# Where layer 1's expert tokens come from: rows gathered by indirect DMA instead of one-hot matmuls, in a two-layer block with 16 experts

## Chip, cores and metric

One core of a Trainium2 chip runs the whole program as one launch. The metric is the device time of that launch in microseconds (us): before the change the median of 3 runs is 1519.34 us (1519.08 to 1524.59). In the profile PE is the matmul engine, DVE the vector engine, ACT the scalar engine, POOL is GpSimd, and SP is the engine that issues most loads.

## What is computed

The reference runs two layers over 512 latent tokens and 256 context tokens of width 1024. Each layer norms the tokens, projects them once into four head groups (pooling, grouped attention, Hyena, MLA), projects the joined result out and adds it. Then comes an expert-choice mixture of experts, which is the part that matters here:

```python
def expert_choice_ffn(h, w_router, w_gate, w_up, w_down):
    b, n, d = h.shape
    cap = EC_CAPACITY * n // N_EXPERTS          # 64 of 512 latent tokens, 32 of 256 context tokens
    aff = jax.nn.softmax((h @ w_router).astype(jnp.float32), axis=-1)
    gate, idx = lax.top_k(jnp.swapaxes(aff, 1, 2), cap)
    xg = jax.vmap(lambda hb, ib: hb[ib])(h, idx)
    a = jnp.einsum('becd,edf->becf', xg, w_gate)
    u = jnp.einsum('becd,edf->becf', xg, w_up)
    y = jnp.einsum('becf,efd->becd', jax.nn.silu(a) * u, w_down) * gate[..., None].astype(h.dtype)
    scatter = lambda ib, yb: jnp.zeros((n, d), h.dtype).at[ib.reshape(-1)].add(yb.reshape(-1, d))
    return jax.vmap(scatter)(idx, y)

for l in range(DEPTH):                          # DEPTH = 2; the context stream is dropped in the last layer
    ...
    x_new = x_new + g2 * expert_choice_ffn(modulate(rms_norm(x_new, norm2_g[l]), sh2, sc2), ...)
    if not last:
        xc = xc + modc[5] * expert_choice_ffn(modulate(rms_norm(xc, norm2_g[l]), modc[3], modc[4]), ...)
```

Each of the 16 experts has 6 MB of float32 weights in a layer (gate, up and down matrices of 1024 x 512).

## The kernel before

Python code with tiles and pools is traced once; a scheduler then puts each engine's instructions in a fixed order, and a tile that opens in room that another pool gave back waits for that pool's last readers. So the code sets the order only in part: where a tile lies, and how many buffers it has, move instructions as well.

**Routing.** `project_out` adds the mixed heads to the rows in `xn` (one pool, 128 x 1024 floats for each block of 128 tokens) and calls `route_part` for every block and quarter of the columns. It sums squares (L1347), makes the inverse norm `rs`, transposes, and adds to the logits (L1371, L1373). In layer 0 it also writes the normed rows to a scratch in DRAM: POOL multiplies the block (L1377, tile `xh`, one buffer) and issues a store of 512 KB (L1378). In layer 1 it returns before that. `route` then takes the top tokens by a chain of small DVE steps (L1435 to L1486) and gives gates, indices, `sidx` for the scatter and, in layer 0 alone, `gidx` for the gather.

**Picking the tokens.** A group is the tokens of two experts, 128 in all (of four for the context). There are two ways. `slot_matrix` and `gather_rows` pick on chip: PE broadcasts the indices (L1505), DVE builds a one-hot matrix (L1509), 64 matmuls of 128 x 128 multiply `xn` by it (L1521), DVE modulates what comes out (L1524). Or `gather` fetches 128 rows of 4 KB from the scratch by an indirect DMA on POOL's queue (L1573, tile `graw`, one buffer), PE transposes them in 8 steps (L1577), ACT and DVE modulate (`modulate`, L1497 and L1495). Layer 0 takes its first latent group on chip and the other seven, and all four of the context, by DMA. Layer 1 takes all eight on chip, so its `xn` stays until the end.

**Experts.** `expert(e)` is a generator; the loop in `moe` steps two of them in turn. Its PE work: 16 gate/up matmuls over the latent tokens, each of two passes (L1607, 32 in the profile), in layer 0 32 over the context tokens (L1618), transposes of the result (L1630, L1633), the down projections (L1642, in layer 0 also L1650). `glu` (L1593, L1594) and the copy to `hTm` (L1636) lie between. `scatter` makes `y` (L1584) and adds it into the output rows by an indirect DMA on POOL's queue (L1586). `nb` buffers for `y`, `sg` and `hTm`: 2 in layer 0, 1 in layer 1, where `y` and the one-hot matrix share one buffer (tag `lpart`).

**Weights.** `expert_loads` gives each expert six loads of 1 MB on SP's queue (L1544), in the order gate, up (first half), gate, up (second half), down, down, into slots of 1 MB: `ring2`, `ringt`, `ring3`, `ring4`. `SLOTS` says how many: layer 1 has 9 in ring2, 3 in ringt, 6 in ring3 and 2 in ring4, 20 in all. SP takes its queue in order, so one load that waits for its slot holds back all behind it.

Of the kernel before, what the change touches and what calls it, by code (L numbers as in the profile page):

```python
# [17 lines left out]
D = 1024  # L18
# [13 lines left out]
# ---------------------------------------------------------------- layout on the host  # L32
def blocks_(a):
    """rows in blocks of at most 128 partitions"""
    k, n = a.shape
    return np.ascontiguousarray(a.reshape(k // 128, 128, n).transpose(1, 0, 2).reshape(128, -1)).astype(np.float32)
# [138 lines left out]
# ---------------------------------------------------------------- the program  # L175
# the slots of the "ring2" pool in the order of their use, and how many slots "ring3" and "ring4" have
SLOTS = ([0, 1, 4, 2, 5, 3], 5, 4), ([0, 1, 2, 7, 8, 3, 4, 5, 6], 6, 2)
EARLY = 3, 9
LATE_STEPS = ((1, 0), (1, 2), (2, 0), (2, 2))
# which engine takes a step: vector (v), gpsimd (p) or scalar (a)  # L180
# [5 lines left out]
class Pipe:  # L186
    """side work, emitted a step at a time between the steps of the main work"""
# [18 lines left out]
class Block:  # L206
# [36 lines left out]
    def in_order(self):  # L243
        """the tensor engine takes what is traced inside in the order of the trace"""
# [11 lines left out]
    # ---- pieces  # L256
    def run(self):
# [33 lines left out]
        with self.pool("filt", side="right") as p:  # L291
# [3 lines left out]
            p.tile([128, 2048], F32, name="spare")  # the tiles after it lie clear of hT  # L295
# [29 lines left out]
    def open_layer(self, l):  # L325
        """the tables that a layer needs until its attention is done"""
# [26 lines left out]
    # ---- adaLN vectors  # L353
    def modulation(self, l, first=()):
        """a generator: one step for every 512 of the 6144 columns"""
# [45 lines left out]
    # ---- Hyena filters (weights only) -> spectra in DRAM  # L401
# [14 lines left out]
    def filter_mlp(self, p, k):  # L416
        """both layers at once, a layer on each half of the partitions"""
# [34 lines left out]
    def filters(self, scr, s):  # L452
        """the first layer's, in the given tiles"""
# [13 lines left out]
    def late_filters(self, tiles):  # L467
        """the second layer's, in tiles that the experts' weights take afterwards; a generator"""
# [24 lines left out]
    def filter_spectrum(self, tile, hid, w3, decay, tab, nb, n, spec, sqn, beside=False):  # L493
        """beside: the transforms leave the vector engine alone"""
# [51 lines left out]
    # ---- one layer  # L546
    def layer(self, l, npg, xh):
# [22 lines left out]
        def mla_out():  # L570
            """in the place of the rows of the grouped queries, when they are done"""
# [78 lines left out]
        if not last:  # L650
            mp = mg.__enter__()
# [3 lines left out]
        if not last:  # L655
            xpg.__exit__(None, None, None)
        rings["ring3"], rings["ring4"] = r3, r4g.__enter__()
        if last:
            mp = mg.__enter__()
        self.moe(l, mp, xgp, sel, xg0, A2, B2, last, W, load, len(slots) - early)  # L660
        for o in (xpg, r2g, mg, r4g, xgg) if last else (r2g, r4g, mg, xgg):
            o.__exit__(None, None, None)
# [1026 lines left out]
```

## Time and profile before

| | |
|---|---|
| runs, median (lowest to highest) | 1519.34 us (1519.08 to 1524.59) |
| profiled execution, span | 1520.5 us, 1.2 us above the median |
| PE busy | 1413.6 us, 93% of the span |
| DVE, ACT, POOL busy | 701.2, 493.1, 327.7 us |
| layer 0's experts, first gate matmul to last down matmul | 595.1 to 899.2 us |
| layer 1's experts, the same | 1267.0 to 1510.1 us |
| DMA | 339.7 MB, mean 223 GB/s |

The profile is of one execution; times inside it count from its start. "Busy" is the time in which an engine executes something. The chain of waits follows the work that ended last back from the last instruction. The windows view gives, for stretches of time, each engine's busy time, the clock granted to PE as a share of full speed (PEclk), and the busy share of the 16 DMA engines, which can read slightly over 1.

### The profile page before, as it was taken

What the parts mean: (1) busy time and instruction counts of PE and PEld (TensorE: products, weight loads), DVE (VectorE), ACT (ScalarE), POOL (GpSimd) and SP (SyncE); (2) the same over time, 40 slices, a digit from 0 to 9 for tenths busy, and PEclk for the clock granted to TensorE, in tenths of its full rate; (3) what the DMA queues carried; (4) which work ended last, traced back from release to release, by engine and by line L of the source; (5) the groups of instructions that cost most, each with busy time, mean ns of one, the idle gap of its engine ahead of it and who ended that gap; (6) DMA issues with size and microseconds to landing.
All of it is one profiled execution on the core that took longest, in us unless ns stands there. A gap on an engine that the chain in (4) does not pass through costs nothing.

```text
span 1520.5 us, 24869 instructions
## 1 busy us (share of the span) xinstructions
PE 1413.6 (93%) x9937; PEld 944.3 (62%) x9937; DVE 701.2 (46%) x1893; ACT 493.1 (32%) x1206; POOL 327.7 (22%) x344
## 2 busy tenths in 40 slices
PE   6999999897999989999999969999899969999996
PEld 2577787786778875444433327977778956445541
DVE  3555364778654465122222116685786462222221
ACT  5555333434763342010111026544357330000000
POOL 1420141355110133121221132042521000010101
PEclk8999999998999999999999989999899988999998
DMA  9556745011373078999999380123101766999992
GB/s 385 206 196 224 269 158 222 29 51 40 120 277 125 29 277 340 392 391 397 396 391 382 94 280 33 57 87 136 56 29 35 312 247 280 372 401 406 407 383 28
DMA packets 71012, 339.71 MB, mean 223 GB/s; under 512 B 6913, under 2 KB 22913, under 8 KB 36594
## 3 DMA queue, kind: packets, MB, share of 16 engines
q1 hardware_dynamic: 57488, 305.24, 51.2%
q0 software_dynamic: 11376, 25.89, 6.8%
q10 hardware_dynamic: 2034, 7.00, 1.2%
q8 instruction: 78, 1.28, 0.3%
q14 instruction: 36, 0.29, 0.1%
HBM read 313.50 MB, written 24.61 MB: 222 GB/s over the span
## 4 chain that ended last, share of the span: by engine, by line
PE 80%; DVE 10%; issue 3%; DMA 3%; ACT 2%; POOL 1%; POOLq 0%; ACTq 0%; DVEq 0%
PE b L1607 14%; PE b L804 7%; PE b L1642 7%; PE b L1521 5%; PE b L1618 4%; PE b L1112 3%; PE b L793 3%; PE b L367 3%; PE b L1060 3%; PE b L794 3%; PE b L795 3%; PE b L1300 3%; PE b L1301 3%; PE b L1302 3%; PE b L1135 2%
## 5 line engine op out<-in xcount | busy, mean ns | idle before, releaser
L1607 PE MATMUL b<-ring,xg 128*64 128x512 f32 x840 | 221.9, 596 | 0.0
L1593 ACT ACTIVATE sgl<-b 64x512 f32<-64x512 f32 x32 | 18.9, 591 | 424.1 <-PE b L1607 419.1
L1607 PEld LDWEIGHTS b<-ring,xg 128*64 128x64 f32 x840 | 65.8, 137 | 115.4 <-issue 112.7
L1642 PE MATMUL b<-ring,hTm 128*64 128x512 f32 x448 | 108.9, 616 | 2.3 <-DVE hTm L1636 2.1
L793 PE MATMUL b<-whi,hT 128*128 128x256 f32 (+1 forms) x352 | 101.8, 290 | 0.3 <-DVE h L765 0.3
L794 PE MATMUL b<-wlo,hT 128*128 128x256 f32 (+1 forms) x352 | 99.1, 282 | 0.0
L795 PE MATMUL b<-whi,hT 128*128 128x256 f32 (+1 forms) x352 | 98.8, 281 | 0.0
L804 PE MATMUL b<-hT,whi 128*128 128x512 f32 (+1 forms) x384 | 97.4, 360 | 1.0 <-ACT oT L1259 0.7
L1112 PE MATMUL b<-kop,qop 96*128 96x512 f32 (+3 forms) x360 | 85.9, 369 | 12.7 <-ACT P L1117 10.8
L717 DVE TENSOR_TENSOR wlo<-ringt,whi 128x256 fp32r<-128x256 f32 (+1 forms) x192 | 83.0, 474 | 30.4 <-ACT whi L714 30.0
L714 ACT ACTIVATE whi<-ringt 128x256 fp32r<-128x256 f32 (+1 forms) x192 | 67.4, 403 | 43.2 <-PE b L804 22.4
L1586 POOL DMA_INDIRECT xs<-y,sidx x32 | 50.1, 1565 | 144.9 <-DVE y L1584 129.0
L1117 ACT ACTIVATE P<-b,nm 128x768 f32<-128x768 f32 (+1 forms) x80 | 65.5, 819 | 38.4 <-DVE nm L1114 36.7
L1114 DVE TENSOR_REDUCE nm<-b 128x1 f32<-128x768 f32 (+1 forms) x80 | 67.1, 844 | 22.2 <-PE b L1112 21.3
L1521 PEld LDWEIGHTS b<-onehot,xn 128*128 128x128 f32 x576 | 70.1, 203 | 8.2 <-issue 4.1
L793 PEld LDWEIGHTS b<-whi,hT 128*128 128x128 f32 x352 | 67.2, 191 | 11.5 <-ACT sqm L937 2.5
L804 PEld LDWEIGHTS b<-hT,whi 128*128 128x128 f32 x384 | 64.1, 191 | 16.0 <-issue 2.9
L1521 PE MATMUL b<-onehot,xn 128*128 128x128 f32 x576 | 72.0, 289 | 1.9 <-DVE onehot L1509 1.8
L1112 PEld LDWEIGHTS b<-kop,qop 96*128 96x128 f32 (+1 forms) x360 | 58.4, 200 | 24.2 <-ACT P L1117 13.5
L1586 POOL DMA_INDIRECT out_dram<-y,sidx x16 | 25.1, 1568 | 218.6 <-DVE y L1584 193.9
L1300 PE MATMUL b<-whi,oT 128*128 128x256 f32 x240 | 71.3, 299 | 0.0
L1594 DVE TENSOR_TENSOR sgl<-b,sgl 64x512 f32<-64x512 f32 x32 | 22.2, 693 | 105.3 <-ACT sgl L1593 105.0
(372 smaller groups left out, 2996.1 us busy)
## 6 DMA issues: line engine op xcount, KB each, us to landing
ring<-wd SPq DMA_DIRECT2D x56, 1024.0 KB, 8.6
ring<-wu SPq DMA_DIRECT2D x53, 1024.0 KB, 8.5
ring<-wg SPq DMA_DIRECT2D x52, 1024.0 KB, 8.3
ringt<-wmod SPq DMA_DIRECT2D x46, 1024.0 KB, 6.3
ringt<-win SPq DMA_DIRECT2D x14, 1024.0 KB, 5.0
ringt<-wg SPq DMA_DIRECT2D x12, 1024.0 KB, 8.3
ringt<-wu SPq DMA_DIRECT2D x11, 1024.0 KB, 8.6
ringt<-wout SPq DMA_DIRECT2D x8, 1024.0 KB, 5.1
```

What stands on the lines that cost most here:

```text
L714: nc.scalar.activation(hi, src, AF.Copy)
L717: nc.vector.tensor_tensor(lo, src, hi.bitcast(F32), op=OP.subtract)
L793: nc.tensor.matmul(pt[:, :n], hT[0][:, k, t], hi[k], start=k == 0, stop=False)
L794: nc.tensor.matmul(pt[:, :n], hT[0][:, k, t], lo[k], start=False, stop=False)
L795: nc.tensor.matmul(pt[:, :n], hT[1][:, k, t], hi[k], start=False, stop=k == 7)
L804: nc.tensor.matmul(pt[:, a:b], w[k][:, cs], hT[h][:, k, a:b], start=first and k == 0, stop=end and k == 7)
L1112: nc.tensor.matmul(S[:, s:e], q[a][:K, c], k[b][:K, k0 + s:k0 + e], start=y == 0, stop=y == len(terms) - 1)
L1300: nc.tensor.matmul(pt[:, :256], oT[0][k][:, t], hi[k], start=k == 0, stop=False)
L1521: nc.tensor.matmul(pt[:, 128 * k:128 * k + 128], self.xn[:, b, c:c + 128], oh[:, b], start=b == 0, stop=b == 3)
L1586: nc.gpsimd.indirect_dma_start(out=dst.rearrange("t (h d) -> (t h) d", h=D // n), out_offset=bass.IndirectOffsetOnAxis(ap=S["sidx"][:, e:e ...
L1607: nc.tensor.matmul(pa[64 * j:64 * j + 64], X[:, k, o:o + 64], w[k // 4][:, c], start=k == 0, stop=k == 7, tile_position=(0, 64 * j))
L1642: nc.tensor.matmul(py[64 * j:64 * j + 64], hT[:, f], wd[f // 2][:, d:d + 512], start=f == 0, stop=f == 3, tile_position=(0, 64 * j))
```

## The change

In layer 1 `route_part` writes the normed rows to the scratch too, `route` makes `gidx` there too, and `gather` fetches groups 1 to 7 by indirect DMA as in layer 0; only group 0 is still picked on chip. `xn` is given up after group 0 in both layers, ring4 has 4 slots in layer 1 (22 in all), and `y`, `sg` and `hTm` have two buffers there, with `y` under its own tag. The tile `graw` moves in both layers from the pool `moe` into a pool `raw` that is opened last, after `xn` is given up. Comments and docstrings go, so the lines shift: L1607 becomes L1599, L1618 L1610, L1577 L1569, L1521 L1517, L1642 L1632, L1650 L1640, L1544 L1540, L1573 L1565, L1586 L1578, L1377 L1373.

```diff
-SLOTS = ([0, 1, 4, 2, 5, 3], 5, 4), ([0, 1, 2, 7, 8, 3, 4, 5, 6], 6, 2)
+SLOTS = ([0, 1, 4, 2, 5, 3], 5, 4), ([0, 1, 2, 7, 8, 3, 4, 5, 6], 6, 4)
...
         r3, xgp = r3g.__enter__(), xgg.__enter__()
-        if not last:
-            mp = mg.__enter__()
+        mp = mg.__enter__()
         xg0 = xgp.tile([128, 8, 128], F32, name="xg0", tag="xg0", bufs=2)
         self.gather_rows(self.slot_matrix(rp, sel[0], 0), A2, B2, xg0)
         rpg.__exit__(None, None, None)
-        if not last:
-            xpg.__exit__(None, None, None)
+        xpg.__exit__(None, None, None)
         rings["ring3"], rings["ring4"] = r3, r4g.__enter__()
-        if last:
-            mp = mg.__enter__()
+        rwg = self.pool("raw", side="right")
+        self.rawp = rwg.__enter__()
         self.moe(l, mp, xgp, sel, xg0, A2, B2, last, W, load, len(slots) - early)
-        for o in (xpg, r2g, mg, r4g, xgg) if last else (r2g, r4g, mg, xgg):
+        for o in (r2g, rwg, r4g, mg, xgg):
             o.__exit__(None, None, None)
...
         nc.vector.tensor_tensor(R["lg"][:, j, h], R["lg"][:, j, h], pl[:, 0:16], op=OP.add)
-        if last:
-            return
         xh = p.tile([128, D], F32, name="xh", tag="xh", bufs=1)
...
-        for q in range(0 if l == DEPTH - 1 else rep):
+        for q in range(rep):
...
-        nb = 1 if last else 2
-        xg, picked = {(0, 0): xg0}, {}
+        nb = 2
+        xg = {(0, 0): xg0}
...
             s = S["s"]
-            if last:
-                xg[s, g] = xp.tile([128, 8, 128], F32, name=f"xg{s}", tag=f"xg{s}", bufs=2)
-                self.gather_rows(picked.pop(g), A2, B2, xg[s, g])
-                return
-            raw = p.tile([128, D], F32, name=f"graw{s}", tag="graw", bufs=1)
+            raw = self.rawp.tile([128, D], F32, name=f"graw{s}", tag="graw", bufs=1)
...
-            y = p.tile([128, n], F32, name=f"y{S['s']}", tag="lpart" if last else f"y{S['s']}", bufs=nb)
+            y = p.tile([128, n], F32, name=f"y{S['s']}", tag=f"y{S['s']}", bufs=nb)
...
             load(4)
-            if last and e % 2 == 0 and e + 2 < N_EXP:
-                picked[e // 2 + 1] = self.slot_matrix(p, sel[0], e // 2 + 1)
             for S in sel:
```

What this does to the order of instructions shows at three places. In the rows a name with a number is a tile and its buffer; `b` is an accumulator of PE.

PE at the start of layer 0's experts, before (`graw` are the context's rows, `onehot` the matrix of the first latent group, `xg` the modulated tokens):

```order
L1466 MATMUL b_6138<-cst,idf 128x32
L1472 MATMUL b_6143<-tv,cst 128x16 x2
L1577 MATMUL b_6279<-cst,graw_6277 128x128 x8
L1505 MATMUL b_6184<-cst,ti_6146 128x64 x2
L1521 MATMUL b_6192<-onehot,xn 128x128
...
L1521 MATMUL b_6213<-onehot,xn 128x128 x13
L1607 MATMUL b_6297<-ringt,xg_6183 64x512 x8
L1618 MATMUL b_6317<-ringt,xg_6288 32x256 x6
L1607 MATMUL b_6297<-ringt,xg_6183 64x512
L1607 MATMUL b_6297<-ring_6239,xg_6183 64x512
```

And with the change:

```order
L1462 MATMUL b_6138<-cst,idf 128x32
L1468 MATMUL b_6143<-tv,cst 128x16 x2
L1501 MATMUL b_6184<-cst,ti_6146 128x64 x2
L1517 MATMUL b_6192<-onehot,xn 128x128
...
L1517 MATMUL b_6213<-onehot,xn 128x128 x13
L1599 MATMUL b_6300<-ringt,xg_6183 64x512 x9
...
L1569 MATMUL b_6282<-cst,graw_6280 128x128 x8
L1610 MATMUL b_6320<-ringt,xg_6291 32x256 x4
L1599 MATMUL b_6364<-ring_6248,xg_6183 64x512
```

The 8 transposes of the context's rows stood ahead of the one-hot matmuls; now they stand behind all the latent gate/up matmuls of expert 0.

PE in layer 0 around the latent gate/up matmuls of expert 15 (weights in `ringt`), the `hTm` and `sgl` being those of expert 14, before:

```order
L1630 MATMUL b_8087<-cst,sgl 128x64 x4
L1633 MATMUL b_8087<-cst,sgc 128x64 x2
L1618 MATMUL b_8096<-ringt,xg_7695 32x256 x2
L1642 MATMUL b_8132<-ring_7805,hTm 64x512 x4
L1642 MATMUL b_8132<-ring_7807,hTm 64x512 x4
L1650 MATMUL b_8144<-ring_7805,hTm 32x256 x6
L1607 MATMUL b_8067<-ringt,xg_7929 64x512 x7
L1618 MATMUL b_8096<-ringt,xg_7695 32x256
L1607 MATMUL b_8067<-ringt,xg_7929 64x512
L1618 MATMUL b_8096<-ringt,xg_7695 32x256 x15
L1650 MATMUL b_8144<-ring_7805,hTm 32x256 x2
```

And with the change, from the down projections of expert 13 to those of expert 14:

```order
L1632 MATMUL b_8038<-ring_7659,hTm 64x512 x4
L1632 MATMUL b_8038<-ring_7661,hTm 64x512 x4
L1640 MATMUL b_8050<-ring_7659,hTm 32x256 x8
L1640 MATMUL b_8050<-ring_7661,hTm 32x256 x8
L1599 MATMUL b_8070<-ringt,xg_7932 64x512 x9
...
L1599 MATMUL b_8070<-ring_7850,xg_7932 64x512
L1620 MATMUL b_8090<-cst,sgl 128x64 x4
L1623 MATMUL b_8090<-cst,sgc 128x64 x2
L1610 MATMUL b_8099<-ringt,xg_7698 32x256 x18
...
L1632 MATMUL b_8135<-ring_7808,hTm 64x512 x4
L1632 MATMUL b_8135<-ring_7810,hTm 64x512 x4
```

Before, the gate/up matmuls over latent tokens (L1607) are cut into pieces, with pieces of the previous expert's down projections and of the context's matmuls between them; now one expert's pieces of a kind stand together. Over the 16 experts of layer 0 the latent gate/up matmuls stand in 39 unbroken pieces before and in 17 now, those of the context in 38 and 21, the down projections in 19 and 22 and in 16 and 19.

SP in layer 1, from the last ring3 load on, with what each load waits for in brackets (PE, DVE, Activation and Pool are engines, DMAHW and DMASW transfers of hardware and POOL queues), before:

```order
L1544 DMA ring_12310<-wd 128x2048 [waits DMAHW6_49,DMAHW1_49]
L1544 DMA ring_12312<-wg 128x2048 [waits DMASW4_49,DMAHW2_49,DMASW3_49,DMAHW7_49,DMASW2_49,DMASW1_49]
L1544 DMA ring_12314<-wu 128x2048 [waits DMAHW0_49,Pool_49]
L1544 DMA ring_12339<-wg 128x2048 [waits DMAHW4_49,DMAHW1_49,PE_49]
L1544 DMA ring_12341<-wu 128x2048 [waits DMAHW2_49,PE_49]
L1544 DMA ring_12343<-wd 128x2048 [waits DMAHW3_49,PE_49]
```

And with the change:

```order
L1540 DMA ring_12332<-wd 128x2048 [waits DMAHW6_49,DMAHW1_49]
L1540 DMA ring_12334<-wg 128x2048 [waits DMAHW2_49,DMAHW4_49,PE_49,DMAHW7_49,Activation_49,Pool_49]
L1540 DMA ring_12336<-wu 128x2048 [waits DMAHW0_49,DVE_49]
L1540 DMA ring_12338<-wg 128x2048 [waits DMASW7_49,DMASW4_49,DMAHW1_49,DMASW3_49,DMASW0_49]
L1540 DMA ring_12340<-wu 128x2048 [waits DMAHW2_49]
L1540 DMA ring_12365<-wd 128x2048 [waits DMAHW3_49,PE_49]
L1540 DMA ring_12367<-wd 128x2048 [waits DMAHW4_49,PE_49]
```

Before, the first ring4 load waits for DMAs alone, the second for POOL, and the third load shown waits for PE, for a slot that expert 0 has read. Now there are four ring4 loads; the first waits for PE, whose last reading of `xn` is group 0's one-hot matmuls, the third for the stores of the normed rows, and the first that waits for a slot read by expert 0 is the fifth.

## Rows read from the trace of the kernel before

**Rows 1.** The page, the chain of work that ended last, by engine.

```profile
PE 80%; DVE 10%; issue 3%; DMA 3%; ACT 2%; POOL 1%; POOLq 0%; ACTq 0%; DVEq 0%
```

**Rows 2.** Windows: stretch, us, busy PE, PEld, DVE, ACT, POOL, PEclk, DMA share, GB/s.

```profile
730.00:837.00 107.00, 106.62 (x835) 41.47 (x832) 23.70 (x48) 13.88 (x30) 21.91 (x16) 1.00 1.03 387
837.00:899.00 62.00, 60.61 (x464) 21.82 (x458) 9.20 (x21) 3.97 (x11) 15.68 (x27) 1.00 0.52 170
1296.00:1475.00 179.00, 178.10 (x1014) 88.97 (x1014) 45.52 (x107) 7.10 (x12) 17.06 (x11) 1.00 1.02 400
```

**Rows 3.** Chain of waits, layer 0, experts 1 to 3: start, us, what.

```profile
617.56 1.03 PE b L1577 x8
...
624.04 7.02 PE b L1607 x32
...
640.61 7.02 PE b L1607 x32
```

**Rows 4.** The same chain, layer 0, experts 13 to 15.

```profile
837.45 3.58 PE b L1607 x14
...
857.54 3.58 PE b L1607 x14
...
861.66 1.00 PE b L1607 x2
...
878.05 3.58 PE b L1607 x14
```

**Rows 5.** Timeline of PE, the last down matmuls of layer 0's experts.

```profile
897.25 1.93 PE L1650 MATMUL b<-ring,hTm 128*32 128x256 f32 x32
```

**Rows 6.** Chain of waits, layer 0, group 0's one-hot matmuls.

```profile
585.58 9.56 PE b L1521 x64
```

**Rows 7.** Chain of waits, layer 1: group 0, and groups 5 and 6.

```profile
1256.91 10.08 PE b L1521 x64
...
1402.84 7.38 PE b L1521 x64
...
1432.80 7.34 PE b L1521 x64
```

**Rows 8.** Timeline of SP, layer 1: loads issued (the first and last of a long row).

```profile
1253.05 0.33 SPq L1544 DMA_DIRECT2D ring<-wu  x1
1270.60 0.33 SPq L1544 DMA_DIRECT2D ring<-wg  x1
...
1471.70 2.81 SPq L1544 DMA_DIRECT2D ring<-wd  x2
```

**Rows 9.** DMA, 1296 to 1475: queues (packets, MB, share), issues (KB, us to landing).

```profile
q1 hardware_dynamic: 9405, 68.49, 92.6%
q0 software_dynamic: 1584, 2.88, 8.7%
...
ringt<-wd SPq DMA_DIRECT2D x6, 1024.0 KB, 7.5
out_dram<-y,sidx POOLq DMA_INDIRECT x11, 9.2
```

**Rows 10.** Timeline of DVE beside POOL, layer 0's top tokens.

```profile
581.70 2.00 DVE L1479 TENSOR_TENSOR md<-md,mm 128x16 f32<-128x16 f32 x1
```

**Rows 11.** Timeline, the end of layer 1.

```profile
1504.71 5.35 PE L1642 MATMUL b<-ring,hTm 128*64 128x512 f32 x16 [0.52 <-DVE hTm L1636]
...
1511.13 1.56 POOL L1586 DMA_INDIRECT out_dram<-y,sidx  x1 [12.83 <-DVE y L1584]
```

**Rows 12.** Windows near the end of layer 1, columns as in rows 2.

```profile
1485.00:1490.00 5.00, 3.17 (x16) 1.01 (x12) 1.07 (x3) 0.59 (x1) 0.40 (x1) 1.00 0.40 52
1490.00:1495.00 5.00, 4.90 (x16) 1.60 (x18) 0.70 (x2) 0.00 (x0) 1.56 (x1) 0.66 0.39 51
1495.00:1500.00 5.00, 5.00 (x26) 1.58 (x22) 0.75 (x1) 0.00 (x0) 1.56 (x1) 1.00 0.25 23
```

**Rows 13.** DMA, 789 to 805, layer 0: a gather's issue (KB left out, us to landing).

```profile
graw<-xh,gidx POOLq DMA_INDIRECT x1, 12.7
```

## The prediction

> **What bounds the kernel now.** I read the chain of waits by engine first: PE has 80% of it [rows 1], so the question is in which stretches PE's own instructions set the pace, and what takes over there when they get fewer. The windows answer it by stage [rows 2]. From 730 to 837 (layer 0's experts) PE is busy 106.62 of 107.00 us, and the DMA share is 1.03: both are full. From 837 to 899 PE is busy 60.61 of 62.00 while the DMA share falls to 0.52, part of which is already the next layer's loads: here PE alone sets the end. From 1296 to 1475 (layer 1's experts) it is again both, 178.10 of 179.00 and 1.02. The granted clock is 1.00 in all three, the 2.4 GHz level. So the chain of waits has to tell what PE spends its time on.
>
> In layer 0 an early expert takes 640.61 - 624.04 = 16.57 us [rows 3], and 1.03 more where a gathered group's 8 transposes fall into it. The late ones take 857.54 - 837.45 = 20.09 and 878.05 - 857.54 = 20.51 [rows 4], without any transposes and for the same matmuls. The rows show why: the 32 latent gate/up passes that take 7.02 us in one piece [rows 3] appear as 14 in 3.58 us and 2 in 1.00 us [rows 4], and 14 cost 3.58 also where 16 together would cost half of 7.02, or 3.51. A piece that is broken off costs its time twice over: each break between kinds of matmul is worth up to 1.00 us.
>
> In layer 1 a pair of experts takes 1432.80 - 1402.84 = 29.96 us, of which the one-hot matmuls are 7.38 [rows 7]. SP issues its 20th load at 1253.05, the next at 1270.60, and the last pair at 1471.70 [rows 8]; with a landing of 7.5 us [rows 9] all weights are there near 1482, but PE ends at 1504.71 + 5.35 = 1510.06 [rows 11]. PE carries a backlog of 28 us.
>
> **Layer 0: the order.** The diff moves only `graw` to another pool there, but that changes PE's order for all 16 experts: 39 pieces of latent gate/up matmuls become 17, and 38 of the context's become 21. I count from expert 2, which starts at 624.04. Before, PE ends at 897.25 + 1.93 = 899.18 [rows 5], 275.1 us later. With the change:
> - 14 experts at 16.57: 232.0.
> - 9 gathered groups left of 11, at 1.03: 9.3.
> - Three experts that are still broken once: nothing to 1.00 each; I take 0.45, since most of these breaks leave long pieces, so 1.4.
> - After the last context gates only the last expert's transposes, copy and down projections remain. These are 1.93 [rows 5], half of 7.02 for the latent half, and about 1 for the rest: 6.5.
>
> That is 249.2. The start costs something. Before, the context's 8 transposes stood ahead of the one-hot matmuls that begin at 585.58 [rows 6], where PE waited for the top tokens anyway. Now `graw` lies in `xn`'s room, so the gather goes out only after the one-hot matmuls end at 595.14, and the transposes stand behind expert 0's latent gates, 7.02 us later, with nothing beside them on PE. I price the transposes at 1.03, the wait for landing and modulation at 1.6 and two breaks at 0.45, together 3.5. The bounds are 1 (transposes alone) and 8 (a landing of 12.7 [rows 13] less the 7.02 of cover, and two whole breaks). So expert 2 starts at 627.5 and PE ends at 876.7, 22.5 us earlier. I take off 1.5 for gathers that land late in other experts: **-21**. The ends are -10, if half of the late experts' extra time has another cause, and -24.
>
> Do the loads allow it? In 18.2 us 387 GB/s [rows 2] move what I count for an expert: 6.29 MB of weights and some 0.75 MB of gathers and scatters. PE would need 16.57 + 0.64 = 17.2. Loads are thus slower by 1 us an expert, but they lead: the share falls at 837, some 60 us before PE ends, and 22 us less leaves them ahead.
>
> **Layer 1: what goes.** Seven groups' one-hot matmuls go from PE: 7 x 7.38 = 52 us, and their slot matrices, one-hot builds and DVE evacuations. In come 7 x 8 transposes, 7.2 us by the row of layer 0 [rows 3]. An expert then needs (29.96 - 7.38)/2 + 0.5 = 11.8 us of PE, 16 of them 189, from 1267 to 1456. But the loads cannot follow: from the queue's share [rows 9] 179 x 0.926 us for 68.49 MB makes 2.54 us a load, 2.50 when the share of 1.02 is scaled to 1. An expert's six loads take 15.0, its scatter 179 x 0.087/11/1.02 = 1.39, its half gather some 0.6: 17.0 us. **Loads become the bound** from about expert 7 on, and the sum is theirs, from the moment at which they restart:
> - Group 0's matmuls end at 1256.91 + 10.08 = 1266.99 [rows 7]. The first ring4 load now waits for them, as the first gather does. Before, the restart was at 1270.60 [rows 8].
> - The top tokens come later where POOL's fourth multiply of normed rows stands beside DVE's chain. A DVE step of 128 x 16 took 2.00 us beside POOL's work in layer 0 [rows 10]. Nothing to 2.0; I take 1.0, as one such meeting is to be expected and it need not be a full one. Restart at 1268.0.
> - The normed rows' multiplies and stores lie beside this chain, while the loads stand still; the casts for `gidx` lie beside PE's broadcast. Both cost nothing. Without that cover the four stores of 512 KB would cost half a load each, 5.0.
> - 18 loads are in by then, the 20 of before less ring4's two. 78 x 2.50 = 195.0.
> - 7 gathers. By bytes each is half a load, 1.25; as two scatters of 256 KB it is 2.8. I take 1.4, near the load, since it moves rows of 4 KB and adds nothing into memory: 9.8.
> - 15 scatters ahead of the last load, 20.9; and one load's time, 2.5, until the stream runs.
> - Last landing at 1268.0 + 228.2 = 1496.2. Then half the last down projection: 1.8 to 2.7 (half of 5.35 [rows 11]); I take 2.7. From PE's end to the scatter's issue 1511.13 - 1510.06 = 1.07, and from there to the end of the span 9.37 [rows 11].
>
> End at 1509.3 against 1520.5: **-11.2** (-14 to 0). What is late next is the loads, so the second buffers of `y`, `sg` and `hTm` are worth nothing by themselves; without them a DMA-paced PE would wait for the scatter's landing of 9.2 us [rows 9], which 17.0 us an expert would hide. For the gather the Trainium skill ("DMA: Bandwidth & Descriptors", Anatomy of one DMA) fits 2.0 us plus the bytes at 436 GB/s, an estimate of 3.2 us for 512 KB. By that the gathers would take 12.6 us more. The same fit would give 2.6 for a scatter, and rows 9 show 1.39.
>
> PE's order in layer 1's attention and Hyena stage changes too, without any added work: 0, from -5 to +5.
>
> **Sum.** 1520.5 - 21 - 11.2 = 1488.3 for a profiled span. That of before is 1.2 above the median of the runs, so on their scale **1487**.
>
> **Rivals.**
> - *Loads pace layer 0* (0.11). If experts took 18.2 us whatever PE's order, layer 0 would stay as it is or lose the 3.5 of the start: 1508 to 1512. For it speaks the share of 1.03 up to 837; against it that the slow experts lie after 837, where the share is 0.52.
> - *Layer 1 gives nothing* (0.13). The gathers cost 2.8 each in the full stretch (9.8 more), or SP, behind the wait for the stores of the normed rows, restarts later than I think: 1498. For it speaks a gather's landing of 12.7 us [rows 13]; against it that a landing is latency, and PE has 5 us to spare in each expert.
> - *The clock falls* (0.06), the slower one. Once PE waits for loads in every expert, its granted clock could drop. After the stretch from 1485 to 1490, in which PE was busy 3.17 of 5.00 us, the clock was 0.66 in the next 5 us and 1.00 again in those after [rows 12], and the down projection took 5.35 us [rows 11] where 3.5 is usual. One such drop costs 1.8 us, and PE has 17.0 - 11.8 = 5.2 to spare, so it decides only if some 10 us of each expert run at the lower level of 1.2 GHz. If all of them did, experts 8 to 15 would take 23.6 each: 1268 + 8 x 11.8 + 8 x 23.6 + 10.4 = 1562, less layer 0's 21 and the 1.2, 1539. Against it: a PE that falls behind the loads no longer waits for them, and the clock returns. The Trainium skill ("TensorE: Matmul & The Clock Gate", HAM oscillation — how this bites in real kernels) speaks for it: there a kernel that waited for a DMA between bursts began every burst at the lower clock. By that rule alone each expert loses a part, which the 5.2 us take in.
>
> **How the numbers follow.** My forecast has 0.70. The range of 1477 to 1506 takes in the ends of the terms (-24, -14 and -5 together give 1476) and the second rival; the first and the third, 0.17, stay outside. A measurement of this kernel can tell about 0.5%, or 7.6 us, from no change: 1511.7 is the border. Faster by more: 0.70 + 0.13 and half of the first rival, less a little for a bad order in the attention stage, 0.85. Within it: 0.09. Slower: the clock, 0.06.
>
> **What the profile would show.** Right: layer 0's last down matmul near 877; experts 3 to 15 at 16.6 or 17.6 us in the chain; in layer 1 loads restarting at 1268 - 21, a DMA share of 1 until some 25 us before the end, PE waiting for loads in experts 8 to 15, and DMA rows of `ring` in the chain there. Wrong: layer 0 ending at 890 or later with loads as the releaser of gate matmuls; gathers that release PE's transposes in the chain; a clock below 0.9 over layer 1's second half.

## The result, and the profile after

| | before | after |
|---|---|---|
| median (lowest to highest), 4 runs each | 1519.45 us (1519.08 to 1524.59) | **1497.89 us** (1496.76 to 1505.81) |
| ratio, 95% interval | | **0.9846** [0.9818, 0.9875] |
| profiled span | 1520.5 | 1496.0 |
| start to the first one-hot matmul of layer 0 | 585.6 | 587.9 (+2.3) |
| from there to layer 0's last down matmul | 313.6 | 295.7 (-17.9) |
| from there to layer 1's first one-hot matmul | 357.7 | 361.8 (+4.1) |
| from there to the end of the span | 263.6 | 250.6 (-13.0) |

The change gains 21.6 us between the medians, where 32 were forecast. The four stretches below the span add up to it, so the last column says where the 24.5 us between the two profiles lie: both expert stages gain, and the stage between them loses. Some 3 us of the 24.5 are no gain: every run on record takes some 2 us more than its span, so the profiled execution of before, with its 1520.5, was some 3 us slower than the median of its runs, and the profiled 1496.0 was not.

The page of the changed kernel:

```profile
span 1496.0 us, 24010 instructions
...
PE 1354.0 (91%) x9517; PEld 900.8 (60%) x9517; DVE 687.9 (46%) x1839; ACT 505.9 (34%) x1234; POOL 341.4 (23%) x359
```

PE is busy 60 us less than before and the span is 24.5 us shorter: the rest of what was taken from PE has become waiting. The windows say where (stretch, us, busy PE, PEld, DVE, ACT, POOL, PEclk, DMA share, GB/s):

```profile
607.00:612.00 5.00, 3.60 (x20) 1.59 (x22) 1.23 (x3) 1.54 (x4) 0.95 (x1) 0.74 0.66 238
612.00:617.00 5.00, 5.00 (x36) 1.68 (x36) 0.41 (x1) 0.29 (x1) 0.00 (x0) 0.92 1.02 425
730.00:837.00 107.00, 106.43 (x972) 45.29 (x964) 25.20 (x50) 14.96 (x32) 23.72 (x17) 1.00 1.03 393
...
1296.00:1475.00 179.00, 151.99 (x659) 53.15 (x656) 31.16 (x59) 16.22 (x33) 24.34 (x17) 0.92 1.02 403
...
1465.00:1470.00 5.00, 4.21 (x14) 1.47 (x16) 0.65 (x2) 0.00 (x0) 0.00 (x0) 0.66 1.05 364
1470.00:1475.00 5.00, 5.00 (x25) 1.68 (x22) 0.75 (x1) 0.00 (x0) 1.56 (x1) 1.00 1.00 424
```

Against [rows 2]: layer 0's middle reads as before (106.43 of 107.00 busy), yet more matmuls fit in, 972 records for 835. In layer 1 PE is busy 151.99 of 179.00 where it was 178.10, and the DMA share stays at 1.02: the loads pace this stage now.

The timeline of layer 0's experts shows the gain and what was paid for it (start, us, engine, line, operation; in brackets the idle time before it and what ended that):

```profile
596.16 1.11 POOL L1373 TENSOR_SCALAR xh<-xn,rs 128x1024 f32<-128x1024 f32 x1 [9.16 <-DVE xg L1520]
597.57 0.60 POOL L1374 DMA_DIRECT2D xh<-xh  x1 [0.30 <-POOL xh L1373]
598.58 1.05 POOL L1565 DMA_INDIRECT graw<-xh,gidx  x1 [0.41 <-DVE xg L1520]
...
607.85 1.06 PE L1569 MATMUL b<-cst,graw 128*128 128x128 f32 x8 [3.43 <-DMA graw<-xh,gidx]
...
610.47 5.65 PE L1599 MATMUL b<-ring,xg 128*64 128x512 f32 x18
...
858.38 1.93 PE L1640 MATMUL b<-ring,hTm 128*32 128x256 f32 x32
...
874.95 1.93 PE L1640 MATMUL b<-ring,hTm 128*32 128x256 f32 x32
...
881.68 1.93 PE L1640 MATMUL b<-ring,hTm 128*32 128x256 f32 x32
```

A late expert takes 874.95 - 858.38 = 16.57 us, the same as an early one and not the 20 of [rows 4]. But the first gather is issued at 598.58 and PE waits 3.43 us for it. Behind that wait the granted clock is 0.74 and then 0.92, and 18 gate passes take 5.65 us; as many took 4.51 in one piece before, on the full clock (timeline of PE):

```profile
710.34 4.51 PE L1607 MATMUL b<-ring,xg 128*64 128x512 f32 x18
```

Layer 1, the timeline of PE, SP and POOL:

```profile
1245.45 10.09 PE L1517 MATMUL b<-onehot,xn 128*128 128x128 f32 x64 [0.50 <-DVE onehot L1505]
1255.67 0.33 SPq L1540 DMA_DIRECT2D ring<-wg  x1
...
1472.84 0.33 SPq L1540 DMA_DIRECT2D ringt<-wd  x1
...
1483.10 1.89 PE L1632 MATMUL b<-ringt,hTm 128*64 128x512 f32 x8
...
1486.07 1.56 POOL L1578 DMA_INDIRECT out_dram<-y,sidx  x1 [11.90 <-DVE y L1576]
```

The loads restart right behind the one-hot matmuls (1245.45 + 10.09 = 1255.54), and their last is issued 217.2 us later. Before, the last pair was issued at about the same time, from 1471.70 on [rows 8], but PE then worked until 1510.06 [rows 11]; now it is done at 1483.10 + 1.89, some 12 us behind the last issue. PE's waits between 1256 and 1484 (what waited, for what: us in total, times, longest):

```profile
PE b L1632 <- DVE hTm L1626: 13.1, 10, 3.1
PE b L1620 <- DVE sgl L1586: 9.0, 7, 1.4
PE b L1569 <- DMA graw<-xh,gidx: 4.0, 1, 4.0
PE b L1599 <- DMA ring<-wg: 3.3, 3, 2.1
```

That is 29 us of waiting, most of it for the glu steps between an expert's gate and down matmuls (`sgl`, `hTm`), and only 3.3 for a weight load. By the DMA share the loads set the pace, by this view DVE's steps do. The runs below separate the two, and show them nearly even.

### The profile page after: what moved, and what is told of

The parts are those of the page before. It is cut to its first block, busy times and chain, and to the rows that moved or that the text cites. A ratio compares the mean times of both kernels' runs of the same rounds, so it can differ in the third digit from the quotient of the medians.

```text
span 1496.0 us, 24010 instructions
## 1 busy us (share of the span) xinstructions
PE 1354.0 (91%) x9517; PEld 900.8 (60%) x9517; DVE 687.9 (46%) x1839; ACT 505.9 (34%) x1234; POOL 341.4 (23%) x359
## 5 line engine op out<-in xcount | busy, mean ns | idle before, releaser
L1599 PE MATMUL b<-ring,xg 128*64 128x512 f32 x824 | 213.6, 600 | 3.3 <-DMA ring<-wg 3.3
L1599 PEld LDWEIGHTS b<-ring,xg 128*64 128x64 f32 x824 | 67.3, 139 | 116.5 <-issue 111.8
L1632 PE MATMUL b<-ring,hTm 128*64 128x512 f32 x464 | 119.4, 637 | 13.3 <-DVE hTm L1626 12.6
L1110 PE MATMUL b<-kop,qop 96*128 96x512 f32 (+3 forms) x360 | 86.0, 369 | 13.5 <-ACT P L1115 11.6
L1632 PEld LDWEIGHTS b<-ring,hTm 128*64 128x64 f32 x464 | 34.2, 145 | 75.9 <-issue 58.7
L1115 ACT ACTIVATE P<-b,nm 128x768 f32<-128x768 f32 (+1 forms) x80 | 65.4, 818 | 39.4 <-DVE nm L1112 37.6
L1586 DVE TENSOR_TENSOR sgl<-b,sgl 64x512 f32<-64x512 f32 x32 | 22.2, 693 | 121.9 <-ACT sgl L1585 121.6
L1578 POOL DMA_INDIRECT xs<-y,sidx x32 | 50.6, 1582 | 120.3 <-DVE y L1576 112.5
L792 PEld LDWEIGHTS b<-wlo,hT 128*128 128x128 f32 x352 | 68.7, 195 | 3.2 <-issue 2.5
L1138 ACT ACTIVATE PT<-b 128x384 f32<-128x384 f32 (+1 forms) x140 | 57.6, 448 | 37.7 <-PE b L1133 36.9
```

The lines of the kernel that those rows point to most:

```text
L792: nc.tensor.matmul(pt[:, :n], hT[0][:, k, t], lo[k], start=False, stop=False)
L1110: nc.tensor.matmul(S[:, s:e], q[a][:K, c], k[b][:K, k0 + s:k0 + e], start=y == 0, stop=y == len(terms) - 1)
L1115: nc.scalar.activation(P[:, :n], S[:, :n], AF.Exp, bias=nm, accum_out=sm)
L1599: nc.tensor.matmul(pa[64 * j:64 * j + 64], X[:, k, o:o + 64], w[k // 4][:, c], start=k == 0, stop=k == 7, tile_position=(0, 64 * j))
L1632: nc.tensor.matmul(py[64 * j:64 * j + 64], hT[:, f], wd[f // 2][:, d:d + 512], start=f == 0, stop=f == 3, tile_position=(0, 64 * j))
```

## The experiments

In the table L0 is from the first one-hot matmul of layer 0 to its last down matmul, "middle" from there to layer 1's first one-hot matmul, L1 from there to the end of the span, each from the profiled execution (us). The ratio is to the kernel before on the same chip.

| run | median | ratio [95%] | L0 | middle | L1 |
|---|---|---|---|---|---|
| before | 1519.45 | | 313.6 | 357.7 | 263.6 |
| after | 1497.89 | 0.9846 [0.9818, 0.9875] | 295.7 | 361.8 | 250.6 |
| e1_raw_last_only | 1509.34 | 0.9906 [0.9876, 0.9936] | 295.3 | 365.1 | 264.3 |
| e2_raw_as_before_l0 | 1512.25 | 0.9929 [0.9899, 0.9959] | 313.7 | 358.1 | 255.9 |
| e3_order_only | 1500.46 | 0.9862 [0.9826, 0.9898] | 288.0 | 361.9 | 260.4 |
| e4_order_and_l1 | 1493.03 | 0.9812 [0.9774, 0.9850] | 288.1 | 362.2 | 250.7 |
| e5_gather_twice | 1508.01 | 0.9889 [0.9852, 0.9926] | 295.8 | 364.4 | 258.5 |
| e6_two_ring4_slots | 1500.88 | 0.9839 [0.9801, 0.9878] | 295.6 | 362.1 | 249.5 |
| e7_single_buffers_l1 | 1501.59 | 0.9850 [0.9815, 0.9886] | 298.0 | 363.1 | 250.7 |
| e8_ring4_before_moe | 1492.35 | 0.9801 [0.9764, 0.9837] | 288.0 | 362.0 | 253.1 |
| e9_order_both_layers | **1483.96** | **0.9761** [0.9736, 0.9785] | 288.5 | 360.8 | 245.2 |
| e10_order_both_old_ring | 1492.71 | 0.9814 [0.9787, 0.9840] | 288.3 | 362.2 | 251.3 |
| after_again (after, unchanged) | 1498.07 | 0.9854 [0.9829, 0.9878] | 295.5 | 362.9 | 252.4 |

**One part alone: `graw` moved in layer 0.** The kernel before, with layer 0's gathered rows in a pool of their own that is opened last:

```diff
+        else:
+            rwg = self.pool("raw", side="right")
+            self.rawp = rwg.__enter__()
...
-            raw = p.tile([128, D], F32, name=f"graw{s}", tag="graw", bufs=1)
+            raw = self.rawp.tile([128, D], F32, name=f"graw{s}", tag="graw", bufs=1)
```

> The kernel before, with one part of the change: in layer 0 alone the tile graw lies in a pool opened last; layer 1 is untouched. Theory (layer 0's gain is PE's order, which this move alone brings): layer 0 as in the changed kernel, expert 2 to the end of the experts 249 to 250 us instead of 275, its start about 8 us later, PE waiting 3 to 4 us for the first graw, so some 17 us less in all: 1501 to 1505 us. Rival (the late experts of the kernel before are slow for another reason, such as what layer 1's part of the change does to loads): no change, 1517 to 1521 us.

L0 is 295.3, as in the changed kernel, and layer 1 stays at 264.3. So this one allocation makes layer 0's whole gain. The time missed its forecast, 1509.34 for 1501 to 1505: the 18.3 us of layer 0 came, but the stretch between the layers lost 7.4 of them (it is taken up at the end). The timeline of PE has the cost too, a wait of 3.00 us for the first gather:

```profile
603.77 1.06 PE L1580 MATMUL b<-cst,graw 128*128 128x128 f32 x8 [3.00 <-DMA graw<-xh,gidx]
...
606.19 5.92 PE L1610 MATMUL b<-ring,xg 128*64 128x512 f32 x18
```

**That part undone.** The changed kernel, with layer 0's `graw` back in the pool `moe`:

```diff
-            raw = self.rawp.tile([128, D], F32, name=f"graw{s}", tag="graw", bufs=1)
+            raw = (self.rawp if last else p).tile([128, D], F32, name=f"graw{s}", tag="graw", bufs=1)
```

> The changed kernel, with graw of layer 0 put back into the pool moe as before; layer 1 keeps all of the change. Theory: layer 0's experts take 275 us from expert 2 again with a start of 38.5 us, so layer 1 alone is left of the change, 13 us less than the kernel before on layer 1's experts, less the 3 us that its attention stage loses: 1507 to 1512 us. If layer 1's part alone brought the whole gain: 1498 us.

L0 is back at 313.7 and the middle at 358.1. The two parts add up: against the kernel before on the same chip e1 gains 13.5 us and this one 10.6, together 24.1, and the whole change 21.6. Layer 1 gained 7.7 by its own stretch here (255.9 for 263.6), less than in the changed kernel, because the end is longer: 27.7 us from the last load's issue to the end of the span, where it is 23.2 there. The changed kernel run again lies between, with 25.8 and an L1 of 252.4; so differences of 2 us in L1 between single profiles say nothing. What makes the end longer is told behind the last runs. The time, 1512.25, lies at the upper end of what was expected.

**Order without the late gather.** The kernel before, with PE told to take layer 0's experts in the order in which they are written, and the context's next gather written behind the next expert's latent gates:

```diff
+                if e and e % 4 == 0:
+                    gather(sel[1], e // 4)
...
-            for S in sel:
-                if (e + 1) % S["rep"] == 0 and e + 1 < N_EXP:
-                    gather(S, (e + 1) // S["rep"])
+            if (e + 1) % 2 == 0 and e + 1 < N_EXP:
+                gather(sel[0], (e + 1) // 2)
...
+            if not last:
+                ordered.enter_context(self.in_order())
```

> The kernel before, graw where it was and layer 1 untouched; the only edit is that PE takes layer 0's experts in the order in which the program is written (one expert's matmuls of a kind together, a context group's transposes behind the next expert's latent gates). Theory: the order alone is worth 24 to 26 us from expert 2 on, without the late first graw: 1493 to 1498 us. Rival (loads pace layer 0, whatever the order): 1517 to 1521 us. In between, 1503 to 1512 us, if the waits for gathers or for the results of ACT and DVE that the scheduler's order hid come back.

`graw` lies where it lay, so the first gather is early. The timeline of PE shows the first one-hot matmuls and the last down matmuls of layer 0:

```profile
587.67 1.65 PE L1521 MATMUL b<-onehot,xn 128*128 128x128 f32 x6 [0.51 <-DVE onehot L1509]
...
873.77 1.93 PE L1651 MATMUL b<-ring,hTm 128*32 128x256 f32 x32
```

L0 is 288.0, so the order of PE's instructions, with the context's gathers moved along, is worth 313.6 - 288.0 = 25.6 us by itself, with the same matmuls, loads and number of gathers as before. The 295.3 of e1 is 7.3 longer, and all of that lies ahead of expert 2, which starts 45.7 us behind the first one-hot matmul instead of 37.6: that is the price of the first gather that has to wait for `xn`'s room, with the breaks that its place in the order brings. The time, 1500.46, missed the 1493 to 1498 that were expected, again by what the stretch between the layers lost, 4.2.

**The same order under the changed layer 1** (e2 with the edit of e3):

> The changed kernel with graw of layer 0 in the pool moe as before and PE taking layer 0's experts in the order in which the program is written. Theory (the two layers' gains add): 25 us of layer 0, 13 of layer 1, less the 3 that its attention stage loses: 1482 to 1487 us, below both kernels. If the late first graw costs nothing on the way to the end: 1495 to 1499 us, as the changed kernel.

288.1 and 250.7: in the two stages the gains stand side by side, and the price of the late gather that the change pays is gone. This kernel is 0.9812 of before. Its 1493.03 missed the 1482 to 1487 that were expected: 29.8 us came on its chip instead of 35. The stretch between the layers lost 4.5 and not 3, and the rest lies ahead of the experts, with 590.4 us to the first one-hot matmul for 585.6.

**A second gather.** The changed kernel with single buffers (e7, below) leaves room for a tile `twin`, into which layer 1 fetches each group a second time; nothing reads it:

```diff
+            if last:
+                twin = self.rawp.tile([128, D], F32, name="twin", tag="twin", bufs=1)
+                nc.gpsimd.indirect_dma_start(out=twin, out_offset=None, in_=self.xh[s],
+                                             in_offset=bass.IndirectOffsetOnAxis(ap=S["gidx"][:, g:g + 1], axis=0))
```

> The kernel with single buffers in layer 1 (the run beside it), in which each of layer 1's seven gathers is followed by a second one of the same rows into a tile that nobody reads. Against that run: theory (loads pace layer 1, and a gather takes 1.4 us of the DMAs' time): 9.8 us longer, all of it between the restart of the loads and the last one. At the price of two scatters, 2.8 each: 20 us longer. Rival (PE or POOL's queue paces layer 1, the transfers are hidden): 0 to 3 us longer.

The first and last load of the stage on SP's timeline, and the DMA issues between 1270 and 1470 (count, median us to landing):

```profile
1256.71 0.33 SPq L1540 DMA_DIRECT2D ring<-wg  x1
...
1480.90 0.33 SPq L1540 DMA_DIRECT2D ringt<-wd  x1
```

```profile
twin<-xh,gidx POOLq DMA_INDIRECT x6, 11.0
graw<-xh,gidx POOLq DMA_INDIRECT x6, 10.6
```

And SP's timeline of its control, e7:

```profile
1262.07 0.33 SPq L1540 DMA_DIRECT2D ring<-wg  x1
...
1479.51 0.33 SPq L1540 DMA_DIRECT2D ringt<-wd  x1
```

The load stream is 224.2 us long against 217.4, and L1 258.5 against 250.7. Seven gathers cost 6.8 us of stream, 1.0 each. The other runs of the changed layer 1 have streams of 216.1 to 218.1, so it is 0.9 to 1.2. That a transfer which nothing reads makes the stream longer is what loads that set the pace do. The end follows only in sum: PE ends 9.1 us behind the last landing where it is 3.6 in e7, partly on a granted clock of 0.66, and the span ends 7.6 us behind PE where it is 11.0. Between the medians it is 6.4, with runs of e5 from 1500.43 to 1511.42. A gather's landing takes 10.6 us here, ten times its price. The Trainium skill ("DMA: Bandwidth & Descriptors", Anatomy of one DMA) would put 512 KB at 3.2 us by its fit, an estimate; seven would be 22 us, and this run does not bear that out as a price in a full stream.

**Four slots, and second buffers, each taken away from the changed kernel:**

```diff
-SLOTS = ([0, 1, 4, 2, 5, 3], 5, 4), ([0, 1, 2, 7, 8, 3, 4, 5, 6], 6, 4)
+SLOTS = ([0, 1, 4, 2, 5, 3], 5, 4), ([0, 1, 2, 7, 8, 3, 4, 5, 6], 6, 2)
```

> The changed kernel with two slots in ring4 in layer 1 instead of four. Theory (loads pace layer 1 from their restart behind the one-hot matmuls, and PE runs ahead of its slots): from the first one-hot matmul to the end 250 to 253 us, as in the changed kernel (250.5), so 1497 to 1501 us. Rival (the room given to the ring is what layer 1 gains): two loads fewer in flight at the start and waits for slots later, 255 us or more, over 1502 us.

```diff
-        nb = 2
+        nb = 1 if last else 2
```

> The changed kernel with one buffer each for y, sg and hTm in layer 1, as before, y under its own tag. Theory (a PE paced by loads has some 5 us to spare in each expert): from the first one-hot matmul to the end 250 to 252 us, 1497 to 1500 us. Rival (the scatter's landing of 9 us holds the next y, and so PE and the slots): 256 us or more.

L1 is 249.5 and 250.7 against 250.6, the ratios 0.9839 and 0.9850 against 0.9846. Neither the two more slots nor the second buffers are worth anything that can be measured here.

**Earlier loads.** In e8 the four slots of ring4 are opened ahead of the pool `moe`, where no one-hot matmul has to end first (on the base of e4; its slots are used in another order):

```diff
-            rest += [(f"ring{i}{j}", 1) for j in range(n)] if last else [(f"ring{i}", n)] * n
+            rest += [(f"ring{i}{j}", 1) for j in ((3, 0, 2, 1) if i == 4 else range(n))] if last else [(f"ring{i}", n)] * n
...
+            for j in range(n4):
+                first[f"ring4{j}"] = rings["ring4"].tile([128, 2048], F32, name=f"ring4{j}", tag=f"ring4{j}")
+            mp = mg.__enter__()
```

> The kernel of e4 (order of layer 0 as written, graw where it was, layer 1 as changed), with ring4 opened ahead of the pool moe in layer 1 and its four slots used in the order 3, 0, 2, 1, so that none lies in the room of xn and the first three lie in room that is free before the top tokens are known. Theory (the loads' restart sets layer 1's end, each us of it one us): no idle of the DMAs of 8 us around the one-hot matmuls, from the first one-hot matmul to the end 243 to 245 us instead of 250.7, so 6 to 8 us less than e4: 1483 to 1488 us where the kernel before takes 1520 to 1523. Rival (the gathers behind the one-hot matmuls, or PE's backlog of three experts, set the end): as e4, 250 us.

This missed. From the first one-hot matmul the last load is issued after 220.0 us instead of the 227.7 of e4, 7.7 sooner, and yet L1 is 253.1 for 250.7 and no shorter. The span ends 33.1 us behind the last load's issue:

```profile
1455.43 0.33 SPq L1546 DMA_DIRECT2D ringt<-wd  x1
```

PE's waits from 1245 to 1478 have no load among the first three:

```profile
PE b L1639 <- DVE hTm L1633: 12.4, 10, 3.1
PE b L1627 <- DVE sgl L1592: 11.3, 8, 1.4
PE b L1575 <- DMA graw<-xh,gidx: 8.3, 1, 8.3
```

So with the loads sooner PE is the bound, through its own order: an expert's transposes (L1627) and down matmuls (L1639) mostly stand right behind its gates, and PE waits out the glu steps each time. The first gather, issued into full DMA queues, adds 8.3.

**The order in layer 1 too.** e9 is e8 with the written order, in both layers. There an expert's transposes stand between the two halves of the next expert's gate matmuls and its down matmuls behind both, so that its glu steps run beside gates; e10 is e4 with the same:

```diff
-            if not last:
-                ordered.enter_context(self.in_order())
+            ordered.enter_context(self.in_order())
```

> The kernel of e8 (ring4 ahead of moe), with PE taking layer 1's experts too in the order in which the program is written: the next expert's gate/up matmuls stand between the results of one expert and its down projection. Theory (in e8 the loads are done 7.5 us sooner, and PE's waits for ACT and DVE, some 2 us an expert, and its wait of 8 us for the first gather took their place as the bound): these waits go, and from the first one-hot matmul to the end it takes 244 to 248 us instead of 253.1, 5 to 9 us less than e8. If the end is set by something behind PE: 250 us or more.

> The kernel of e4 with the same order of PE in layer 1, ring4 where the change has it. Theory (in e4 and in the changed kernel the loads set the pace and end within PE's reach): next to nothing, from the first one-hot matmul to the end 248 to 251 us (e4: 250.7). If PE's own waits already bind in the changed kernel: 245 us or less.

With the early ring the order is worth 253.1 - 245.2 = 7.9 us; with the old ring it gives nothing, 251.3 against 250.7. PE's waits in e10 have only moved, from 24.7 us for `hTm` and `sgl` in e4 to 25.5 for `ring` and `ringt`: there the loads come later anyway. PE's waits in e9 from 1240 to 1490 are for loads now, and the glu steps are down to 2.7 us:

```profile
PE b L1605 <- DMA ring<-wu: 13.9, 11, 2.0
PE b L1605 <- DMA ringt<-wu: 3.1, 2, 1.8
PE b L1605 <- DMA ring<-wg: 2.1, 3, 0.7
PE b L1627 <- DVE sgl L1592: 1.4, 1, 1.4
PE b L1639 <- DVE hTm L1633: 1.3, 2, 0.8
```

e9 is the fastest kernel of the study, 1483.96 us. On the same chip the changed kernel took 1498.07 and the kernel before 1521.91.

**Which of the two ends layer 1.** Expert 15's last up weights are first read by the 19th of its 32 gate passes. In the profiles of the changed kernel, e4, e6, e7, e9 and e10 that pass starts 0.04 to 0.12 us behind their landing: there the loads end the stage. In the changed kernel run again it starts 2.9 us behind, in e5 3.2, in e2 4.5, in e8 10.5 and in the kernel before 22.6: there PE does. So in the changed kernel the two are nearly even. Timelines of PE, of the changed kernel run again (expert 14's down and expert 15's gate matmuls, no wait between them) and of e10 (PE waits for that load), and the window of e10 that stands against 1296 to 1475 above:

```profile
1467.68 5.28 PE L1632 MATMUL b<-ring,hTm 128*64 128x512 f32 x16 [0.52 <-DVE hTm L1626]
1472.79 7.03 PE L1599 MATMUL b<-ring,xg 128*64 128x512 f32 x32
```

```profile
1468.26 3.65 PE L1600 MATMUL b<-ring,xg 128*64 128x512 f32 x14 [1.01 <-DMA ring<-wu]
```

```profile
1288.00:1467.00 179.00, 153.62 (x660) 51.92 (x656) 31.06 (x59) 16.57 (x33) 22.77 (x16) 1.00 1.02 403
```

## Why the prediction was right, and where it was off

The forecast was 1487 us, from 1477 to 1506; measured were 1497.89, inside the range and on the side forecast, with two thirds of the gain. Of the some 11 us between them the start of layer 0 has 4.2, the stretch between the layers 3.1 (1.0 of it had been priced), the time ahead of layer 0's experts 2.3 and the step from span to median 3.1; layer 0's later gathers and layer 1 give back 1.9.

- **Layer 0's order: right.** From expert 2's start to the last down matmul it said 249.2 us for the 275.1 of before. Measured: 634.05 to 881.68 + 1.93, or 249.6. The reading of [rows 3, 4], that pieces broken off cost their time twice, is borne out by e3, where the order alone gave 25.6.
- **Layer 0's start: the term that was too small.** It put the transposes, the wait for landing and modulation and two breaks at 3.5 us, between 1 and 8. From the first one-hot matmul expert 2 starts 634.05 - 587.88 = 46.17 us later, before 624.04 - 585.58 = 38.46 [rows 3, 6]: 7.7 us, near the upper bound. PE's waits of 3.43 and 0.55 were priced at 1.6: the gather goes out 1.2 us behind the one-hot matmuls (598.58, they end at 597.40), and PE starts on it 9.3 us later. What was not priced is the clock behind that wait, 1.1 us over the next 18 passes. The 1.5 us for later gathers landing late, on the other hand, did not come up: PE's waits of layer 0 name `graw` once.
- **The top tokens: off, on the safe side.** The 1.0 us for POOL's multiply beside DVE's chain did not appear. From DVE's copy ahead of the first MAX8 of the last top-k to the one-hot matmuls it is 14.77 us in both profiles.
- **Layer 1: the size right within 2 us, PE's part wrong.** The term was -11.2, or -12.2 from the first one-hot matmul; measured were -13.0, and -11.2 with the changed kernel run again. Loads as the new bound, their restart behind group 0's matmuls, and the worthless second buffers (e7) came as said. A gather was too dear, 1.0 and not 1.4 (e5), which is most of why the stream from restart to last landing took some 225 us, not 228.2. What failed is PE's slack: 17.0 - 11.8 = 5.2 us an expert. Measured, six loads take 16.7 us (217.2/78 x 6) and PE is idle 27.0 of 179 us, 2.5 an expert, most of it for `sgl` and `hTm`, waits that do not appear in the working. So the sign named for a right forecast, PE waiting for loads in experts 8 to 15, did not come: 3.3 us in three waits. That the time fits all the same is partly luck, since both chains end together: e10 removes PE's waits and gains nothing, e8 brings the loads sooner and gains nothing, e9 does both.
- **The middle: the term taken as 0 was +4.1,** inside its bounds of -5 to +5. Some 3 us lie from the first transposes of attention's probabilities to the first output projection. Windows of this stretch, columns as above, of before, the changed kernel, e3 and e1:

```profile
1079.01:1182.17 103.16, 98.21 (x888) 86.38 (x886) 73.55 (x142) 63.36 (x155) 29.96 (x30) 0.98 0.14 50
1064.14:1170.29 106.15, 98.49 (x887) 86.55 (x886) 72.83 (x142) 63.80 (x155) 29.78 (x30) 0.98 0.13 48
1058.43:1162.67 104.24, 99.28 (x888) 87.25 (x886) 73.54 (x142) 63.28 (x155) 30.00 (x30) 0.97 0.13 48
1061.93:1169.78 107.85, 100.18 (x888) 87.68 (x886) 72.90 (x142) 63.87 (x155) 29.80 (x30) 0.97 0.13 47
```

The runs fall into groups here: those with `graw` in the late pool in layer 0 share an order of PE that is not that of before, and take 105.9 to 107.9; e2 and those with PE's order written out have the order of before in this stretch, and take 102.9 to 104.4. Within each group the lower times go with a granted clock of 0.98 and the higher with 0.97. In the four rows PE is idle 7.7 us with the new order and 5.0 with that of before, at either clock. So what was done in layer 0 shifted the order a stage later, and that goes with some 3 us. No run set this order by itself, so that it is the cause is not shown.

- **2.3 us lie ahead of layer 0's one-hot matmuls:** PE's order is the same up to there but for the context's eight transposes, and over all the kernels run that point lies anywhere from 583.4 to 592.5 (585.6 before; 587.9 and 586.1 in the two profiles of the changed kernel).
- **From span to median: 1.2 us were taken off, 1.9 came on top.** The median of the changed kernel lies 1.9 above its profiled span. A run's time is some 2 us more than its span, so a forecast of a span had to go up and not down.

The rivals: *loads pace layer 0* fell, since PE is busy 106.43 of 107.00 and late experts take 16.57. *Layer 1 gives nothing* fell by its own price, 1.0 for 2.8. *The clock falls* shows, and costs little: from 1296 to 1475 the mean is 0.92 where it was 1.00, with 0.66 in 1465 to 1470 and 1.00 again in the next 5 us. The loads still end the stage in that profile, and e10, at 1.00 over the like stretch, is no faster. In the changed kernel run again, where PE ends the stage, expert 14's down matmuls take 5.28 us where 3.65 is the full clock's, so there the lower clock has a share of up to 1.6 us. The Trainium skill ("TensorE: Matmul & The Clock Gate", HAM oscillation) describes bursts that begin at the lower clock behind a wait for a DMA; the trace agrees that bursts begin so, here behind PE's waits for the glu steps.

## What to carry to other kernels

Before asking what a stage's work costs, compare two repeats of the same work in the trace: experts of 16.6 and of 20 us with identical matmuls meant that their order was the cost, and the largest gain here came from a moved buffer that only changed that order. A buffer that is placed in room freed late makes its first fill late as well, so the first use is to be costed by the row of a landing, with the slow clock behind the wait. When a bound is removed, look at the waits that were hidden under it before removing the next one: here two bounds lay even, so that earlier loads were worth nothing until PE's order was set too, and the order nothing without earlier loads. Whether the last load or the engine ended a stage shows in the first instruction that reads it: it starts right behind the landing, or well behind.

## What the runs showed that had not been expected

**POOL beside DVE is not always a loss.** The timeline of layer 1's top tokens, and of the same stage of layer 0:

```profile
1238.24 0.41 DVE L1453 FIND_INDEX8 idx<-vals,tk 32x8 uint32<-32x256 f32 x1
1238.46 1.11 POOL L1373 TENSOR_SCALAR xh<-xn,rs 128x1024 f32<-128x1024 f32 x1 [8.66 <-DVE tk L1452]
1238.58 0.40 DVE L1450 MAX8 vals<-tk 32x8 f32<-32x256 f32 x1
```

```profile
583.47 1.27 POOL L534 TENSOR_TENSOR ring<-ring 128x512 f32<-128x512 f32 x1
...
584.02 1.99 DVE L1475 TENSOR_TENSOR md<-md,mm 128x16 f32<-128x16 f32 x1
```

MAX8 and FIND_INDEX8 keep their 0.40 and 0.41 us beside POOL's multiply, and the multiply keeps its 1.11, while a small TENSOR_TENSOR beside POOL's TENSOR_TENSOR takes 1.99; the same one takes 0.17 in layer 1, where POOL is idle. The prediction had carried the second over to the first.

**The price of a gather is a tenth of its landing.** In a stream of loads at a share of 1.02 a 512 KB gather lands 9 to 11 us after its issue and takes 0.9 to 1.2 us from the stream, no more than the 1.25 that its bytes would take at the loads' own rate of 2.50 us for 1 MB.
